# Layer 1 of a two-layer decoder step in two token groups, and the sample group's value sums in two fp32r passes over split pages

## The chip, the cores and the metric

The kernel runs on one core of one Trainium2 chip. The metric is device time in microseconds of one execution, input and output in HBM. The time before is 2708.54 us, the median of three runs (2706.16 to 2709.74).

## The reference

One inference step of a two-layer causal decoder (model width 1024) for two request groups that share one set of weights: a prompt of 1024 tokens, and eight sample requests of eight tokens each (64 rows) that have 1024 past tokens in a paged cache of keys and values (8 pages of 128 tokens per request, found through a page table). All data is fp32.

```python
for layer in range(DEPTH):                       # 2 layers
    hn = rms_norm(h, norm_mix_g[layer])
    if layer % 2 == 0:   # conformer convolution (width 31) | stick-breaking attention, 8 heads x 64
        mix = conformer_sb_mixer(hn, ...)        # w_in_even 1024 x 2560, w_out_even 1024 x 1024
    else:                # gated convolution (width 3) | causal pooling, windows 2/4/8/16
        mix = shortconv_pool_mixer(hn, ...)      # w_in_odd 1024 x 2048, w_out_odd 1024 x 1024
    h = h + mix
    h = h + swiglu(rms_norm(h, norm_ffn_g[layer]), w_ffn_in[layer], w_ffn_out[layer])   # 2816 wide
y = rms_norm(h, norm_final_g)

# stick-breaking attention of one block of queries
z = einsum('nqhd,nkhd->nhqk', q, k) * scale + bias
mask = k_pos < q_pos
log_1m = where(mask, log_sigmoid(-z), 0)
after = lax.cumsum(log_1m, axis=3, reverse=True) - log_1m
wgt = exp(where(mask, log_sigmoid(z) + after, -inf))
out = einsum('nhqk,nkhd->nqhd', wgt, v)
```

It also returns the new keys and values and the last rows of every convolution and pooling input.

## The kernel before

**Layout.** The residual stream lies in SBUF as `hb`, 128 channels by 8 blocks by 1088 token columns (1024 prompt, 64 sample). `Grp` names a set of columns and the width of one matmul: GA is the prompt's columns 0 to 511, one matmul of 512; GB the columns 512 to 1087 with the sample group at the end, two matmuls of 288; GT all 1088, three matmuls of 364, 364 and 360.

**Projections.** A product of fp32 numbers is made of fp32r numbers: every operand is split into a high part and a remainder, and `mm3` (L167) adds high x high, high x low and low x high, three passes per 128x128 block of the weight. Weights come as tiles of 512 KB (128 x 1024): `w_load` (L138) issues their DMAs on the SyncE queue into three `stage` buffers, `w_split` (L146) lets ScalarE (ACT) copy the high part (L152) and GpSimd (POOL) subtract for the low part (L153) into three `hl` buffers; both run a few tiles ahead of the matmuls. The list `seq` fixes the order of the tiles. A tile makes 8 x 3 = 24 passes (`block`, `pair`), or 4 x 2 x 3 in the second FFN matrix (`out_block`, L347). VectorE (DVE) takes the accumulators out: `scaled` (L226) multiplies by the norm's factor, `added` (L230) adds to `hb`. `run_in` (L280) runs an input projection with a function per output block, `run_out` (L315) an output projection that also prepares the next operand (`prep`, L302, with its low part on DVE at L307), `run_ffn` (L352) the SwiGLU. There `ev_u` gives a product to POOL (L378) and the split of the result to ACT and DVE (L175, L176) through `post`, a list that `flush` (L234) works off in the middle of the next block.

**Order.** The instructions are issued in the order of the program text, each engine's queue in order. Layer 0: the input projection for A, then for B (0 to 348 us); then output projection and FFN for A (348 to 1097), then for B (1097 to 1577). `to_mixer` (L1207) is the end of B's FFN: it adds the last products and prepares the operand of layer 1 for all 1088 columns. Layer 1 runs once for GT (1577 to 2658): input projection with its mixer (L1251 to L1353), output projection, FFN. `to_y` (L1366) ends the last FFN block by block with the final norm and the transposes to rows.

**Background.** Attention, convolution and the sample group run between the matmuls of a projection. They are generators that give back control after each piece; the projections call a `slot` at fixed places (L248, L260, L385 to L388, L412), and `bg` (L266) then issues one piece of the list `flow`. In group A's layer 0 this is `flow_c` (L1157): attention of group B (`attention`, L756: scores, `s2` with the scans on DVE at L815 to L820, transposes at L830, sums at L839), then the convolution of B (`conv_b`, taps at L693) alternating with the sample group, then the norm of the convolution. `last_a` (L1180) ends A's FFN and first issues what is left of the flow without gaps (`drain`).

**The sample group** (`sample`, L870): units of two or three pages of one request; `trans` transposes the key pages (L928) and splits them (L931, L932), `score` multiplies (L951), `weights` scans, `weights_t` transposes the weights in nine blocks (L1000), and `pv` sums the values: one fp32 matmul per page (L1012) of 64 weight columns and 512 value columns, and one for the new tokens (L1018) per request. Keys come one page to a buffer, values two.

## Time and profile before

| what | value |
|---|---|
| median of three runs | 2708.54 us |
| profiled execution, whole | 2708.54 us |
| its span, first to last instruction | 2706.8 us |
| mean granted TensorE clock | 0.987 |
| TensorE matmul busy | 2603.3 us (96%) |
| DVE / ACT / POOL busy | 1212.3 / 868.3 / 1031.1 us |
| HBM read / written | 198.09 / 18.69 MB |

The page gives the busy time of every engine in one profiled execution. A group of instructions is named by its line in the kernel, its engine and its operation, with `out<-in` by the program's names, the number of records, the busy time, the mean of one record, and the idle time just before them with what ended it. An fp32 matmul leaves two records. Matmuls overlap in the array, so a record's duration is longer than the distance to the next start. PEld is the loading of stationary operands, which overlaps.

### The profile page before, as it was taken

The numbers are of one execution on the slowest core, as the hardware profiler recorded it, in microseconds if no ns is written. First come the engines' busy times: TensorE is split into PE (matmuls) and PEld (weight loads), VectorE is DVE, ScalarE is ACT, GpSimd is POOL, SyncE is SP. The second block draws the span as 40 slices with busy tenths as digits, with TensorE's granted clock in tenths as the row PEclk, the third lists the DMA queues.
The fourth block names the chain that finished last, engine by engine and source line by source line (L and its number), as shares of the span: only waits on it lengthen the run. The fifth ranks groups of instructions, "written<-read, shape, count | busy, mean of one in ns | idle before, by whom it ended". The sixth has DMA issues, their size and how long they took to land. (4 is left out here: it accounts for less than half of the span.)

```text
span 2706.8 us, 37823 instructions
## 1 busy us (share of the span) xinstructions
PE 2603.3 (96%) x15423; PEld 2365.3 (87%) x15423; DVE 1212.3 (45%) x1730; ACT 868.3 (32%) x1326; POOL 1031.1 (38%) x589
## 2 busy tenths in 40 slices
PE   8989998998999998999999989999999999999997
PEld 6788876887666656899999989999999999999997
DVE  4774776868677642322222243343122222222226
ACT  4436765653433323332222232132211111111112
POOL 5655243343333337464444442224222222222222
PEclk9999999999999999999999999999999999999999
DMA  6432231234444432422222221131111111111111
GB/s 198 123 96 78 66 99 40 62 90 133 144 137 146 120 110 70 136 86 86 79 86 87 79 91 47 43 106 47 39 48 39 47 47 40 48 47 40 47 39 67
DMA packets 293380, 218.75 MB, mean 81 GB/s; under 512 B 21505, under 2 KB 248961, under 8 KB 293192
## 3 DMA queue, kind: packets, MB, share of 16 engines
q1 hardware_dynamic: 293176, 216.33, 26.8%
q8 instruction: 122, 2.00, 0.3%
q14 instruction: 50, 0.41, 0.1%
q10 hardware_dynamic: 32, 0.01, 0.0%
HBM read 198.09 MB, written 18.69 MB: 80 GB/s over the span
## 5 line engine op out<-in xcount | busy, mean ns | idle before, releaser
L153 POOL TENSOR_TENSOR hl<-stage,hl 128x1024 fp32r<-128x1024 f32 x278 | 679.5, 2446 | 1209.9 <-ACT hl L152 816.6
L170 PE MATMUL acc<-x1t,hl 128*128 128x364 f32 (+1 forms) x4896 | 824.1, 330 | 7.1 <-DVE hb L230 6.5
L170 PEld LDWEIGHTS acc<-x1t,hl 128*128 128x128 f32 x4896 | 817.2, 189 | 9.2 <-ACT x1t L304 6.7
L170 PE MATMUL acc<-x,hl 128*128 128x288 f32 (+1 forms) x4704 | 804.3, 325 | 12.9 <-DVE hb L230 9.6
L170 PEld LDWEIGHTS acc<-x,hl 128*128 128x128 f32 x4704 | 690.8, 189 | 88.7 <-issue 39.6
L170 PE MATMUL acc<-hid,hl 128*128 128x364 f32 (+2 forms) x3024 | 530.4, 333 | 20.5 <-DVE hb L230 17.5
L170 PEld LDWEIGHTS acc<-hid,hl 128*128 128x128 f32 x3024 | 480.0, 190 | 58.4 <-DVE hb L230 23.2
L152 ACT ACTIVATE hl<-stage 128x1024 fp32r<-128x1024 f32 x278 | 292.1, 1054 | 585.9 <-PE acc L170 318.5
L226 DVE TENSOR_TENSOR tmp<-acc,rr 128x728 f32<-128x728 f32 (+2 forms) x230 | 160.6, 720 | 684.3 <-PE acc L170 681.6
L230 DVE TENSOR_TENSOR hb<-acc,hb 128x728 f32<-128x728 f32 (+2 forms) x368 | 255.3, 720 | 273.2 <-PE acc L170 272.2
L176 DVE TENSOR_TENSOR hid<-tmp,hid 128x512 fp32r<-128x512 f32 (+2 forms) x66 | 60.8, 921 | 201.8 <-ACT hid L175 201.6
L187 POOL TENSOR_TENSOR ss<-ss,tmp 128x512 f32<-128x512 f32 (+2 forms) x55 | 98.4, 1789 | 91.6 <-ACT tmp L186 89.3
L378 POOL TENSOR_TENSOR tmp<-tmp 128x512 f32<-128x512 f32 (+2 forms) x66 | 117.1, 1774 | 29.3 <-ACT tmp L366 28.2
L175 ACT ACTIVATE hid<-tmp 128x512 fp32r<-128x512 f32 (+2 forms) x66 | 53.4, 809 | 230.8 <-POOL tmp L378 230.8
L170 PE MATMUL acc<-x1a,hl 128*128 128x512 f32 x480 | 122.4, 408 | 3.7 <-POOL hl L153 2.3
L366 ACT ACTIVATE tmp<-tmp 128x576 f32<-128x576 f32 (+1 forms) x44 | 39.6, 900 | 256.1 <-DVE tmp L226 256.1
L170 PEld LDWEIGHTS acc<-x1a,hl 128*128 128x128 f32 x480 | 89.9, 191 | 27.1 <-POOL hl L153 3.8
L693 DVE SCALAR_TENSOR_TENSOR cacc<-ext,par,cacc 128x512 f32<-128x512 f32 x120 | 90.1, 751 | 2.3
L364 POOL TENSOR_TENSOR tmp<-tmp 128x512 f32<-128x512 f32 x22 | 31.7, 1439 | 120.3 <-ACT tmp L363 113.1
L839 PE MATMUL o<-wt,vrow 128*64 128x128 f32 x576 | 76.6, 278 | 0.4 <-ACT wt L831 0.4
L818 DVE TENSOR_TENSOR_SCAN q<-q,ones 128x384 f32<-128x384 f32 (+6 forms) x56 | 76.0, 1357 | 2.0
L655 DVE SCALAR_TENSOR_TENSOR cacc<-ext,par,cacc 128x512 f32<-128x512 f32 x100 | 75.4, 754 | 3.0
(222 smaller groups left out, 1880.2 us busy)
## 6 DMA issues: line engine op xcount, KB each, us to landing
stage<-in_w_ffn_in_dram SPq DMA_DIRECT2D x132, 512.0 KB
stage<-in_w_ffn_out_dram SPq DMA_DIRECT2D x66, 512.0 KB
stage<-in_w_in_even_dram SPq DMA_DIRECT2D x40, 512.0 KB
kst<-in_cache_k_dram SPq DMA_DIRECT2D x64, 256.0 KB
vst<-in_cache_v_dram SPq DMA_DIRECT2D x64, 256.0 KB
stage<-in_w_out_even_dram SPq DMA_DIRECT2D x16, 512.0 KB
stage<-in_w_in_odd_dram SPq DMA_DIRECT2D x16, 512.0 KB
park<-hb SPq DMA_DIRECT2D x16, 288.0 KB
```

The source lines that it names most:

```text
L152: act.activation(hl[:, 0], st, AF.Copy)
L153: pool.tensor_tensor(hl[:, 1], st, f32(hl[:, 0]), op=OP.subtract)
L170: pe.matmul(acc[:, b, :c1 - c0], w, x[:, xi, c0:c1], start=first and s == 0, stop=last and s == 2)
L176: dve.tensor_tensor(dst[:, 1], src, f32(dst[:, 0]), op=OP.subtract)
L187: pool.tensor_tensor(ss[:, g.cs], ss[:, g.cs], t[:, :g.n], op=OP.add)
L226: dve.tensor_tensor(d, a, r, op=OP.mult)
L230: dve.tensor_tensor(d, a, d, op=OP.add)
L378: pool.tensor_tensor(t[:, :n], t[:, :n], u[:, :n], op=OP.mult)
L655: dve.scalar_tensor_tensor(acc, i, w, acc, op0=OP.mult, op1=OP.add)
L693: dve.scalar_tensor_tensor(o, i, w, o, op0=OP.mult, op1=OP.add)
L818: dve.tensor_tensor_scan(e, e, ones[:, 0:1].to_broadcast([128, n - 128]), q[:, n - 128:n - 127], op0=OP.mult, op1=OP.mult)
L839: pe.matmul(o, vrow[h][:, j], w[:, j], start=j == 0, stop=j == i)
```

## The change

- **Groups.** GT is gone. Layer 1 runs for GA right after layer 0 of GA, then both layers for GB. The weights of layer 1 (16 + 8 + 66 tiles) stand in the list twice. `mixer1(g, slot)` is the old mixer for one group: for A it keeps the last rows of the convolution and pooling inputs (`ghalo`, `uhalo`) that B starts from. `to_mixer(g, slot)` prepares the operand for one group only.
- **Background.** `flow_c` starts at the same place, but `bg2` issues a piece at every second slot, and the slots of A's layer 1 (and those added to `run_in`) serve it too. The final norm of A's columns becomes a flow of its own (`flow_y`) between B's layer-0 matmuls; `to_y` does B's columns alone, in two blocks of 256 and 320.
- **Deferred work.** The low part of the FFN's split (L176) goes to a list `late` and is issued one flush later. The transposes of keys and values to rows (`rows_out`) are deferred by one flush. In `attention`, the low parts of keys and queries (L781, L784) move from DVE to POOL.
- **Sample group.** Value pages are loaded one to a buffer (three buffers, the first used for the new tokens) and split by ACT and POOL into `vhl` (two buffers). The transposed weights are split too, high and low side by side as 128 stationary columns, so two fp32r matmuls per page make all four products; the result has 128 rows, which the following selection adds up. The new tokens' values stand as high and low in 64 rows each, with one matmul. Key transposes and scores are issued by single head pairs, in three pieces per step instead of two large ones; the nine transposes of the weights in three pieces.

```diff
+        for j, c in ODD:
+            add_in(w_in_odd[0], j * 512 + c * 128)
+        for n in range(8):
+            add_in(w_out_odd[0], n * 128)
+        add_ffn(1)
...
+    late = []
+
     def flush():
-        todo = post[:]
+        todo, low_parts = post[:], late[:]
         post.clear()
-        for f in todo:
+        late.clear()
+        for f in todo + low_parts:
             f()
...
             def fin():
                 pool.tensor_tensor(t[:, :n], t[:, :n], u[:, :n], op=OP.mult)
-                split(dst, t[:, :n])
+                act.activation(dst[:, 0], t[:, :n], AF.Copy)
+                late.append(lambda: dve.tensor_tensor(dst[:, 1], t[:, :n], f32(dst[:, 0]), op=OP.subtract))
             post.append(fin)
...
-                    small.append(lambda c=c: dve.tensor_tensor(k[o, c:c + 512], ks[:, c:c + 512],
+                    small.append(lambda c=c: pool.tensor_tensor(k[o, c:c + 512], ks[:, c:c + 512],
...
+            def split_v(upto):
+                while len(vhl) + vdone[0] < min(upto, 64):
+                    i = len(vhl) + vdone[0]
+                    v = vst.pop(i)
+                    t = vhl[i] = sa.tile([128, 2, 512], FR, name="vhl", bufs=2)
+                    act.activation(t[:, 0], v, AF.Copy)
+                    pool.tensor_tensor(t[:, 1], v, f32(t[:, 0]), op=OP.subtract)
+                    load_v(i + 4)
...
-                    act.activation(t[:, c0:c0 + n], m[:, :n * 128].rearrange("p (c r) -> p c r", r=128), AF.Copy)
+                    mv = m[:, :n * 128].rearrange("p (c b r) -> p c b r", b=2, r=64)
+                    o = wl[:, c0:c0 + n]
+                    act.activation(o[:, :, :, 0], mv, AF.Copy)
+                    dve.tensor_tensor(o[:, :, :, 1], mv, f32(o[:, :, :, 0]), op=OP.subtract)
+                    yield
...
-                pe.matmul(o, wts[bp][:, k, 64 * b2:64 * b2 + 64], vst[i // 2][:, k % 2], start=k == 0, stop=False)
-                if k % 2:
-                    vst.pop(i // 2)
-                    load_v(i // 2 + 3)
+                w = wts[bp][:, :, b2].rearrange("p c s r -> p c (s r)")
+                v = vhl.pop(i)
+                for s in range(2):
+                    pe.matmul(o, w[:, k], v[:, s], start=k == 0 and s == 0, stop=False)
+                vdone[0] += 1
+                split_v(i + 3)
...
+    def to_mixer(g, slot):
+        def f(hh):
+            for o in range(2):
+                h = w_next()
+                for i in range(4):
+                    n = o * 4 + i
+                    a = accs()
+                    out_block(g, a, h, i, hh)
+                    added(g, hb[:, n, g.cs], a)
+                    sp.dma_start(park[:, n, g.cs], hb[:, n, g.cs])
+                    prep(g, x1, n, pc(MIXG + 8 + n), squares=True)
+                    low(1)
+                    slot()
+            low()
+        return f
...
+    def bg2():
+        turn[0] += 1
+        if turn[0] % 2:
+            bg()
...
-    run_out(GA, accs, x1, FFNG, slot=bg)
+    run_out(GA, accs, x1, FFNG, slot=bg2)
+    ffn(GA, to_mixer(GA, bg2), True, bg2)
+    mixer1(GA, bg2)
+    run_out(GA, accs, x1, FFNG + 8, KS, slot=bg2)
...
+    ffn(GA, last_a, True, bg2)
...
+    flow.append(flow_y())
+    run_out(GB, accs, x1, FFNG, slot=bg2)
+    ffn(GB, to_mixer(GB, lambda: None), False, bg2)
+    drain()
+    mixer1(GB, lambda: None)
+    run_out(GB, accs, x1, FFNG + 8, KS)
...
+    ffn(GB, to_y, False, lambda: None)
```

More of the change, by code (lines that the diff above doesn't have):

```diff
@@ L73, in trunk_kernel @@
     gstack = ExitStack()
[L74 removed]
+    tmpp = gstack.enter_context(tc.tile_pool(name="tmpg", bufs=4, side="right"))
     def tmp():
[L77 removed]
+        return tmpp.tile([128, 640], F, name="tmp")
     ident = consts.tile([128, 128], F, name="ident")
@@ L122, in trunk_kernel @@
             add_in(w_in_even[0], 512 * j + c * 128)
+    ODD = [(j, c) for c in range(4) for j in (3, 1, 2, 0)]
     for _ in range(2):
@@ L287, in run_in @@
             end = i == len(evacs) - 3
-            block(g, a, h, x, ks if end else K0, flush)
+            block(g, a, h, x, ks if end else K0, flush, slot)
             if end:
@@ L293, in run_in @@
                 tail[1]()
+        flush()
         flush()
@@ L399, in run_ffn @@
             if q == G:
+                flush()
                 flush()
@@ L890, in sample @@
             pool.memset(f32(qb), 0.0)
-            vnew = sa.tile([128, 512], F, name="vnew")
-            pool.memset(vnew[64:128], 0.0)
+            vn = sa.tile([128, 512], FR, name="vn")
+            vnew = sa.tile([128, 512], F, name="vst", bufs=3)
             sp.dma_start(vnew[0:64], v_s.rearrange("a b q h d -> (a b q) (h d)"))
@@ L920, in trans @@
                 j = (2 * bp + b2) * 8 + 3 * kb
[L921 to L932 removed]
+                load_k(kpages.index(j) + n)
@@ L933, in trans @@
+                t = kth[u, pr, i] = sa.tile([128, 2, 384], FR, name="kth", bufs=2)
+                m = ms()
+                hp = 2 * pr + i
+                for pg in range(n):
+                    pe.transpose(m[:, pg * 128:pg * 128 + 128], kst[j + pg][:, hp * 128:hp * 128 + 128], ident)
+                act.activation(t[:, 0, :n * 128], m[:, :n * 128], AF.Copy)
+                dve.tensor_tensor(t[:, 1, :n * 128], m[:, :n * 128], f32(t[:, 0, :n * 128]), op=OP.subtract)
                 if i and pr:
@@ L1038, in sample @@
             fill_q(0)
-            load_v(2)
             for _ in range(6):
                 yield 1
-            for i in range(2):
-                trans(*steps[0], i)
-                yield 1
+            act.activation(vn[0:64], vnew[0:64], AF.Copy)
+            dve.tensor_tensor(vn[64:128], vnew[0:64], f32(vn[0:64]), op=OP.subtract)
+            split_v(1)
+            split_v(2)
             s = 0
-            while s < len(steps) or chain or pvq or fins:
+            while s <= 3 * len(steps) or chain or pvq or fins:
                 todo = fins[:] + chain.pop(s, [])
@@ L1103, in in_proj @@
             slot()
+        flush()
         flush()
@@ L1151, in trunk_kernel, with ffn @@
+    def ffn(g, last, sig, slot):
+        with tc.tile_pool(name=f"hid{g.c0}", bufs=2, side="right") as hidp:
+            run_ffn(g, accs, ms, hidp, x1, last, sig=sig, slot=slot)
     acc_pool(GA, 3)
-    hstack = ExitStack()
-    hidp = hstack.enter_context(tc.tile_pool(name="hid0", bufs=2, side="right"))
     knew = consts.tile([128, 4, NS], F, name="knew")
@@ L1360, in trunk_kernel, with flow_y @@
-    run_out(GT, accs, x1, FFNG + 8, KS)
+    def flow_y():
+        with tc.tile_pool(name="ya", bufs=1) as yp:
+            y = yp.tile([128, 4, D], F, name="ya")
+            gall = yp.tile([128, D], F, name="galla")
+            sp.dma_start(gall, bass.AP(tensor=norm_final_g.tensor, offset=norm_final_g.offset, ap=[[0, 128], [1, D]]))
+            yield 1
+            norm_cols(ms, D, 0, 4)
+            yield 1
+            for n in range(8):
+                m = ms()
+                for t in range(4):
+                    pe.transpose(m[:, t * 128:t * 128 + 128], hb[:, n, t * 128:t * 128 + 128], ident)
+                dve.tensor_tensor(y[:, :, n * 128:n * 128 + 128], m.rearrange("p (t c) -> p t c", t=4),
+                                  gall[:, None, n * 128:n * 128 + 128].to_broadcast([128, 4, 128]), op=OP.mult)
+                yield 1
+            for t in range(4):
+                act.activation(y[:, t], y[:, t], AF.Copy, scale=rstd[:, t:t + 1])
+                sp.dma_start(y_p[0, t * 128:t * 128 + 128], y[:, t])
+                yield 1
@@ L1425, in to_y @@
         LAG = 2
-        for q in range(24 + LAG):
-            if q < 24:
+        for q in range(16 + LAG):
+            if q < 16:
                 item(q)
             if q >= LAG:
-                turn(q - LAG)
-            if q % 8 == 4 and q > 8:
-                finish(q // 8 - 1)
-        finish(2)
-    with tc.tile_pool(name="hid1", bufs=2) as hidp:
-        run_ffn(GT, accs, ms, hidp, x1, to_y)
+                turn_y(q - LAG)
+            if q == 12:
+                finish(0)
+        finish(1)
```

472 lines of the change are left out of this document (219 added, 253 removed).

## The prediction

> **What bounds it now.** I read the page's busy shares first, then the stages, cut where the projections change their token group (header: busy per engine with instruction count, granted TensorE clock, DMA share, GB/s).
>
> ```profile
> PE 2603.3 (96%) x15423; PEld 2365.3 (87%) x15423; DVE 1212.3 (45%) x1730; ACT 868.3 (32%) x1326; POOL 1031.1 (38%) x589
> ```
> ```profile
> core 0: us, PE busy (x) PEld busy (x) DVE busy (x) ACT busy (x) POOL busy (x), PEclk, DMA share, GB/s
> 0.00:347.80 347.80, 323.45 (x1931) 278.12 (x1931) 214.72 (x318) 183.55 (x325) 181.89 (x145) 0.99 0.38 110
> 347.80:1096.60 748.80, 694.84 (x3260) 512.66 (x3257) 505.87 (x736) 336.00 (x593) 291.16 (x180) 0.97 0.37 108
> 1096.60:1576.90 480.30, 472.04 (x3567) 470.66 (x3567) 142.09 (x184) 135.31 (x161) 237.78 (x115) 1.00 0.30 89
> 1576.90:2657.60 1080.70, 1077.18 (x6437) 1070.15 (x6437) 317.16 (x410) 195.86 (x217) 302.87 (x133) 1.00 0.16 48
> 2657.60:2706.80 49.20, 35.78 (x234) 33.69 (x234) 32.48 (x83) 17.59 (x31) 17.35 (x18) 0.90 0.24 91
> ```
>
> TensorE sets the time in every row. The second is layer 0 of group A (512 columns) with the background flow between its matmuls: attention of B, B's convolution, the sample group. There TensorE stands idle 748.80 - 694.84 = 54.0 us, and a clock of 0.97 costs 0.03 x 748.8 = 22 us more. The third (layer 0 of B) and fourth (layer 1, all 1088 columns) idle 8 and 4 us. So only removed TensorE work, or those 54 + 22 us, can pay.
>
> **Layer 1 in two groups** replaces, for each 128x128 weight block and pass, three matmuls (364, 364, 360 columns) by one of 512 and two of 288. Starts in the timeline give the price of each, and the 360-wide groups the number of passes:
>
> ```profile
> 1042.51 15.64 PE L170 MATMUL acc<-x,hl 128*128 128x512 f32 x66
> 1057.98 1.56 PE L170 MATMUL acc<-hid,hl 128*128 128x512 f32 x6
> ...
> 1215.28 25.54 PE L170 MATMUL acc<-x,hl 128*128 128x288 f32 x192
> 1240.66 12.64 PE L170 MATMUL acc<-hid,hl 128*128 128x288 f32 x96
> ...
> 2007.99 48.15 PE L170 MATMUL acc<-x1t,hl 128*128 128x364 f32 x288
> 2055.98 24.16 PE L170 MATMUL acc<-hid,hl 128*128 128x364 f32 x144
> ```
> ```profile
> L170 PE MATMUL acc<-x1t,hl 128*128 128x360 f32 x1632 | 534.3, 327 | 0.0
> L170 PE MATMUL acc<-hid,hl 128*128 128x360 f32 x480 | 157.8, 329 | 0.0
> ```
>
> A 512 costs 15.47/66 = 0.2344 us, a 288 25.38/192 = 0.1322, a GT matmul 47.99/288 = 0.1666. New: 0.2344 + 2 x 0.1322 = 0.4988; old: 3 x 0.1666 = 0.4999. Over 1632 + 480 = 2112 passes: **-2.3 us**. The narrower matmuls themselves bring nothing.
>
> It loads and splits 16 + 8 + 66 = 90 weight tiles once more:
>
> ```profile
> L153 POOL TENSOR_TENSOR hl<-stage,hl 128x1024 fp32r<-128x1024 f32 x278 | 679.5, 2446 | 1209.9 <-ACT hl L152 816.6
> ```
>
> That is 90 x 2.446 = 220 us of POOL and 47 MB. A tile feeds 24 passes, 5.6 us of TensorE in A and 6.3 in B, so one 2.45 us split is covered: **0**. Without cover it would be these 220 us; in A the POOL also splits 64 value pages (an estimate from this row: half the elements, 1.2 us each, 78 us), well inside its idle time. SP carries the same number of page loads; each waits for a buffer, with weight loads queued behind it, but those run three buffers ahead. **0**, bound below under the rivals.
>
> **Value sums.** A page now takes one fp32 matmul, seen as two records:
>
> ```profile
> 973.01 1.93 PE L1012 MATMUL o<-vst,wts 128*64 128x512 f32 x4
> 974.87 1.67 PE L170 MATMUL acc<-x,hl 128*128 128x512 f32 x6
> ...
> 981.69 1.02 PE L1018 MATMUL o<-vnew,wts 128*64 128x512 f32 x2
> 982.64 1.66 PE L170 MATMUL acc<-x,hl 128*128 128x512 f32 x6
> ```
>
> Two pages take 1.86 us, one 0.93. After: two fp32r passes, whose nearest row is the 512-wide one, 2 x 0.234 = 0.469; saved 0.46 x 64 pages = 29.5. The new tokens: 0.95 to 0.234, eight times, 5.7. **-35.2 us**; bounds -35 and 0, the latter if the passes wait for their splits.
>
> **The background at half the density.** Counted in the code: before, 280 slots in group A's layer 0, each taking one of the flow's 271 pieces. After, A's two layers give 645 slots, every second takes a piece: 322 turns for 285 pieces (the sample loop's steps are finer). The flow ends inside A's last FFN; nothing is left for the drain. What TensorE waited for in the second stage:
>
> ```profile
> PE acc L170 <- DVE hb L230: 26.9, 8, 7.4
> PE m L1000 <- ACT wts L1001: 9.5, 4, 3.7
> PE m L830 <- DVE be L820: 7.5, 5, 3.5
> PE acc L170 <- DVE tmp L226: 2.1, 2, 1.1
> ```
>
> L1000: nine transposes through two PSUM tiles in one piece. They become three pieces: **-9.5**. L830: attention's scans are late; with twice the matmuls between pieces **-6**. The longest L230 wait:
>
> ```profile
> 439.41 5.09 POOL L153 TENSOR_TENSOR hl<-stage,hl 128x1024 fp32r<-128x1024 f32 x2 [0.86 <-ACT hl L152]
> 439.50 5.55 DVE L781 TENSOR_TENSOR kt<-kall,kt 64x512 fp32r<-64x512 f32 x2
> 445.91 4.61 PE L170 MATMUL acc<-x,hl 128*128 128x512 f32 x10 [7.38 <-DVE hb L230]
> ```
> ```profile
> 440.80:451.00 10.20, 5.09 (x12) 4.05 (x13) 8.48 (x6) 3.66 (x5) 6.58 (x4) 0.50 0.35 103
> ```
>
> Two key splits on DVE last as long as two weight splits on POOL, and the accumulator's release queues behind them. The change puts key and query splits on POOL, in order with the weight splits: **-7.4**. The clock then stays at 0.50 for 10.2 us, so a long wait costs about as much again. The Trainium skill's page "TensorE: Matmul & The Clock Gate" (section "What's actually happening") says the same: half clock until about 3.4 us of sustained work. By that price alone a 7.4 us wait would cost 1.7 us more, against the trace's 5.1; I stay with the trace.
>
> The end of A's FFN:
>
> ```profile
> 1068.98 2.34 POOL L153 TENSOR_TENSOR hl<-stage,hl 128x1024 fp32r<-128x1024 f32 x1
> ...
> 1073.24 0.69 DVE L176 TENSOR_TENSOR hid<-tmp,hid 128x512 fp32r<-128x512 f32 x1 [8.77 <-ACT hid L175]
> ...
> 1074.59 10.70 PE L170 MATMUL acc<-hid,hl 128*128 128x512 f32 x36 [5.68 <-DVE hb L230]
> ```
>
> DVE waits for ACT, which waits for POOL behind a weight split; the releases stand behind L176. The change issues L176 one flush later, when its input is long there. Of what is left of the first row (26.9 - 7.4 = 19.5) and the last (2.1) I take **-16**. Sum -39 of 54 idle; the clock share goes with it: **-16** of 22. Bounds for both together: 0 and -76.
>
> **What it adds.** Group A now goes through the layer change and the layer-1 mixer with the background running. In the layer change (old one, B to all columns):
>
> ```profile
> 1565.33 0.75 DVE L230 TENSOR_TENSOR hb<-acc,hb 128x576 f32<-128x576 f32 x1
> 1566.00 1.85 DVE L307 SCALAR_TENSOR_TENSOR x1t<-hb,par,x1t 128x1088 fp32r<-128x1088 f32 x1
> 1576.88 17.03 PE L170 MATMUL acc<-x1t,hl 128*128 128x364 f32 x90 [6.46 <-DVE hb L230]
> ```
>
> DVE's 0.75 + 1.85 = 2.6 a row block exceeded TensorE's 12 x 0.132 = 1.58; it ended in a 6.5 us wait, with half clock about 10. In B now 0.75 + 1.85 x 576/1088 = 1.73: the old 10 becomes 5, **-5**. In A 0.69 + 0.87 = 1.56 and every second block a background piece (1.7 us of DVE, below) make 2.4, against 6 x 0.234 = 1.41 and the piece's 0.4: eight blocks x 0.6 and some half clock, **+7** (bounds 0 and 10, as before). The mixer:
>
> ```profile
> L226 DVE TENSOR_TENSOR tmp<-acc,rr 128x512 f32<-128x512 f32 x54 | 37.1, 687 | 60.2 <-PE acc L170 57.9 <-POOL tmp L364 2.1
> L1255 DVE TENSOR_TENSOR hb<-hb,tmp 128x1088 f32<-128x1088 f32 x4 | 11.5, 2880 | 0.1
> L1294 DVE SCALAR_TENSOR_TENSOR hb<-ext,par,hb 128x1024 f32<-128x1024 f32 x8 | 10.2, 1279 | 0.0
> L693 DVE SCALAR_TENSOR_TENSOR cacc<-ext,par,cacc 128x512 f32<-128x512 f32 x120 | 90.1, 751 | 2.3
> L693 DVE SCALAR_TENSOR_TENSOR hb<-ext,par,hb 128x64 f32<-128x64 f32 x120 | 52.4, 437 | 3.0
> L932 DVE TENSOR_TENSOR kth<-m,kth 128x384 fp32r<-128x384 f32 x64 | 35.0, 552 | 33.3 <-ACT kth L931 33.3
> ```
>
> At 512 columns a channel tile costs DVE 4 x 0.69 + 1.36 (L1255 scaled) + 3 x 0.64 (L1294 halved) + about 4.5 pooling and split operations at 1.0, midway from L176's 0.69 to 1.36: 10.5, four make 42. The 63 slots take 31 pieces: 15 with convolution taps (2 x 0.75 + up to 3 x 0.44, say 2.5) = 38, and 0.5 (L932) in each for the sample = 16. TensorE: the second stage without idle, clock loss and its 8 + 66 tiles (748.8 - 54 - 22 - 74 x 5.63) is 256, less the 35 saved 221, over 271 pieces 0.82 each; 16 x 5.63 + 31 x 0.82 = 115. DVE at 96 of 115, and ACT and DVE queues in order: I take **+15** (bounds 0 and, with two-operand work doubled, +27). Two more changes from one projection to the next under background: **+3**. B's mixer has two sets of waits where there was one: **+3**. In the first 348 us and the tail nothing that sets the end changes.
>
> **Sum** on the profiled span: 2706.8 - 2.3 - 35.2 - 39 - 16 + 7 - 5 + 15 + 3 + 3 = 2637.3. The profiled execution took 2708.5 (1.7 outside the span), which is the median of the runs: **2639 us**, 2.6% faster.
>
> **Rivals.**
>
> *Nearly no stalls* (chance 0.14). The new +7 and +15 do not come, slots being sparse; 2639 - 22 = 2617, and with the rest of the idle 2600. For: B's layer 0 idles 8 us in 480. Against: DVE at 0.83 in the mixer.
>
> *Stalls only move* (0.15). The waits and clock loss stay, -39 - 16 is not earned: 2694. For: 26.9 of the 54 us are releases behind an in-order DVE queue, which the new schedule keeps.
>
> *Value passes wait* (0.07). Each waits for ACT and POOL to split its page behind a weight split; the 35 us turn into waits: 2674.
>
> *Slower: DVE held by POOL* (0.08). At 439.50 two operations of two SBUF operands took 5.55 us where L176 of as many columns takes 0.69 alone, some 1.9 us more each. In A's mixer some 38 such (L1255, L1294, pooling, splits) run while POOL is busy about half the time, and 16 more at the layer changes: 54 x 1.9 = 103, less 115 - 96 = 19 of slack and the +15 already counted: +69, and some 15 of half clock after the long waits: 2723. It decides where DVE passes TensorE's 115 us there, that is, once the two-operand work (42 - 11 = 31) grows by 60%. For: L1255 takes 2.65 ns an element. Against: L1294, with two SBUF operands too, takes 1.25. The Trainium skill's page "GPSIMD Engine Reference" (section "8. Key points") speaks for it: GpSimd shares its SBUF interfaces with VectorE and contends with instructions of two SBUF inputs; the trace agrees at 439.50.
>
> *The change doesn't do as it says*: the flow not used up before the drain, at 2.6 us a piece at most; the count leaves 37 turns over, so it goes into the moving stalls.
>
> **Numbers.** The forecast (2620 to 2665) has 0.52, the rivals the chances above, and 0.04 lies between 2703 and 2714. Some 0.2% is what a measurement of this kernel can tell from no change. Faster 0.88, same 0.04, slower 0.08. The range 2590 to 2697 leaves out the slow rival, no change, and a mixer that costs nothing with all idle gone.
>
> **What would show it.** Page: fp32 value records (128 + 16) gone, 136 matmuls 512 wide at 0.23 us apart; POOL up by some 300 us. Stages: B's two layers near 1.00 clock; A's about 1190 us (2637 less the first 348, B's 162 x 24 x 0.264 + 30, and a tail of 40). Waits: L1000 and the 7.4 and 5.7 us L230 waits gone. Wrong if a wait on DVE above 20 us in total appears in A's mixer, if releases by the page split (POOL) stand ahead of value passes, or if A's clock is still 0.97.

## The result: 0.46% slower

The changed kernel takes 2720.97 us (median of five runs, 2718.35 to 2722.16), the kernel before 2708.54 (here also a median of five): a ratio of 1.0046, 95% interval 1.0031 to 1.0061. Forecast were 2639 us. The profiled execution of the changed kernel took 2720.97 us, its span is 2719.1. One execution of the experiments below, of e4, took 5022 us and is left out of e4's figures. The page's first part:

```profile
PE 2570.9 (95%) x15415; PEld 2289.1 (84%) x15415; DVE 1309.2 (48%) x1810; ACT 1019.4 (37%) x1619; POOL 1417.9 (52%) x838
```

TensorE has less to do than before (busy 2570.9 after 2603.3), and all three other engines more: POOL 387 us, ACT 151, DVE 97. The stages of the changed kernel, with the columns of the prediction's table; A's two layers are rows two to six:

```profile
core 0: us, PE busy (x) PEld busy (x) DVE busy (x) ACT busy (x) POOL busy (x), PEclk, DMA share, GB/s
0.00:353.90 353.90, 324.95 (x1931) 279.71 (x1931) 214.81 (x302) 184.35 (x326) 202.51 (x161) 0.98 0.37 109
353.90:932.00 578.10, 551.00 (x2742) 445.50 (x2742) 380.06 (x450) 270.15 (x445) 314.04 (x196) 0.99 0.34 98
932.00:959.00 27.00, 19.78 (x74) 15.54 (x75) 21.04 (x29) 13.70 (x25) 15.88 (x11) 0.82 0.43 139
959.00:1107.00 148.00, 121.78 (x549) 96.74 (x549) 83.45 (x146) 60.41 (x121) 62.08 (x43) 0.96 0.37 109
1107.00:1587.00 480.00, 463.51 (x2045) 371.67 (x2046) 248.79 (x363) 179.02 (x289) 313.58 (x178) 0.98 0.37 109
1587.00:1612.90 25.90, 10.52 (x35) 6.45 (x34) 15.73 (x16) 9.42 (x16) 9.95 (x7) 0.77 0.41 121
1612.90:2100.60 487.70, 484.06 (x3612) 482.88 (x3612) 144.87 (x196) 132.31 (x157) 226.26 (x108) 0.99 0.29 88
2100.60:2687.40 586.80, 575.70 (x4286) 572.38 (x4286) 181.16 (x256) 158.84 (x221) 263.96 (x125) 1.00 0.29 86
2687.40:2719.10 31.70, 19.57 (x146) 18.20 (x146) 19.28 (x58) 11.22 (x21) 9.67 (x12) 0.86 0.21 75
```

Against the prediction's own stages: the first part takes 353.9 for 348, A's two layers 1612.9 - 353.9 = 1259.0 for about 1190 (its terms give 1193), B's two layers 487.7 + 586.8 = 1074.5 for 1056, the tail 31.7 for 40. So **66 to 69 of the 82 us missing lie in A's two layers**. There TensorE stands idle 1259.0 - 1166.6 = 92 us (the five PE busy times add up to 1166.6), and the clock costs 578.1 x 0.01 + 27.0 x 0.18 + 148.0 x 0.04 + 480.0 x 0.02 + 25.9 x 0.23 = 32 us more. In A's layer 0 before it was 54 and 22. The prediction wanted the two to shrink by 55; with A's layer 1 and its background they grew by 48. (This clock share also counts half clock in which TensorE stood idle. Counted on TensorE's busy time alone, in slices of 0.5 us, it is 22 us, 15 before, and the growth 45.) Three short stretches stand out: the change of layers (932 to 959, clock 0.82), A's mixer (959 to 1107), and A's last sums (1587 to 1613, TensorE busy for 10.5 of 25.9 us).

What TensorE waited for, in the whole run (microseconds in total, number of waits, the longest):

```profile
PE acc L169 <- DVE hb L229: 55.4, 26, 9.1
...
PE acc L169 <- DVE hid L384: 5.4, 3, 4.4
...
PE z L807 <- POOL kt L787: 4.7, 1, 4.7
```

The wait for the nine weight transposes (9.5 us before) is gone, as forecast. The wait for accumulators that `added` has not yet taken out (now L229) has grown from 33.6 us in ten waits to 55.4 in 26, on average 2.1 us.

The longest of them is the one that the prediction meant to remove. The timeline where it stands, at the end of A's first output projection (start, length, engine, line, operation; in brackets the idle time before and what ended it):

```profile
417.39 3.42 POOL L787 TENSOR_TENSOR kt<-kall,kt 64x512 fp32r<-64x512 f32 x2
...
417.88 6.23 DVE L311 SCALAR_TENSOR_TENSOR x<-hb,par,x 128x512 fp32r<-128x512 f32 x3
...
421.10 5.20 POOL L152 TENSOR_TENSOR hl<-stage,hl 128x1024 fp32r<-128x1024 f32 x2 [0.29 <-POOL kt L787]
...
424.03 2.56 DVE L821 TENSOR_TENSOR_SCAN q<-q,ident 128x128 f32<-128x128 f32 x1
426.62 1.82 DVE L824 TENSOR_TENSOR_SCAN q<-q,ones 128x768 f32<-128x768 f32 x1
...
429.55 1.28 DVE L229 TENSOR_TENSOR hb<-acc,hb 128x512 f32<-128x512 f32 x2
...
430.38 1.19 PE L169 MATMUL acc<-x,hl 128*128 128x512 f32 x2 [9.11 <-DVE hb L229]
```

The key splits are on POOL now (L787), but DVE's next operations of two SBUF operands, `prep`'s low parts (L311), take their place: three of them last 6.23 us while POOL works through two key splits and two weight splits (3.42 and 5.20 us, 0.29 between). Behind them stand the scans of attention, and only then the release. The 7.4 us wait became 9.1.

### The profile page after: what moved, and what is told of

It reads as the page before. It is cut to its first block, busy times and chain, and to the rows that moved or that the text cites. A ratio compares the mean times of both kernels' runs of the same rounds, so it can differ in the third digit from the quotient of the medians.

```text
span 2719.1 us, 38898 instructions
## 1 busy us (share of the span) xinstructions
PE 2570.9 (95%) x15415; PEld 2289.1 (84%) x15415; DVE 1309.2 (48%) x1810; ACT 1019.4 (37%) x1619; POOL 1417.9 (52%) x838
## 5 line engine op out<-in xcount | busy, mean ns | idle before, releaser
L169 PE MATMUL acc<-x,hl 128*128 128x288 f32 (+1 forms) x9600 | 1648.8, 329 | 39.2 <-DVE hb L229 25.8
L169 PEld LDWEIGHTS acc<-x,hl 128*128 128x128 f32 x9600 | 1450.6, 190 | 170.9 <-issue 30.5
L152 POOL TENSOR_TENSOR hl<-stage,hl 128x1024 fp32r<-128x1024 f32 x368 | 896.3, 2438 | 847.9 <-ACT hl L151 616.3
L169 PE MATMUL acc<-hid,hl 128*128 128x288 f32 (+1 forms) x3072 | 542.3, 333 | 34.9 <-DVE hb L229 29.5
L151 ACT ACTIVATE hl<-stage 128x1024 fp32r<-128x1024 f32 x368 | 386.0, 1053 | 418.2 <-PE acc L169 208.9
L169 PEld LDWEIGHTS acc<-hid,hl 128*128 128x128 f32 x3072 | 466.4, 189 | 89.6 <-DVE hb L229 38.6
L225 DVE TENSOR_TENSOR tmp<-acc,rr 128x512 f32<-128x512 f32 (+1 forms) x230 | 166.1, 723 | 726.2 <-PE acc L169 722.3
L229 DVE TENSOR_TENSOR hb<-acc,hb 128x512 f32<-128x512 f32 (+1 forms) x376 | 268.1, 721 | 257.0 <-PE acc L169 256.5
L186 POOL TENSOR_TENSOR ss<-ss,tmp 128x512 f32<-128x512 f32 (+1 forms) x69 | 100.1, 1451 | 115.5 <-ACT tmp L185 114.6
L382 POOL TENSOR_TENSOR tmp<-tmp 128x512 f32<-128x512 f32 (+1 forms) x88 | 119.8, 1361 | 17.8 <-ACT tmp L370 17.5
L384 DVE TENSOR_TENSOR hid<-tmp,hid 128x512 fp32r<-128x512 f32 (+1 forms) x88 | 81.1, 922 | 19.7 <-ACT hid L383 19.7
L699 DVE SCALAR_TENSOR_TENSOR hb<-ext,par,hb 128x64 f32<-128x64 f32 x120 | 87.8, 732 | 3.0
L311 DVE SCALAR_TENSOR_TENSOR x<-hb,par,x 128x576 fp32r<-128x576 f32 (+1 forms) x56 | 74.8, 1355 | 19.9 <-ACT x L308 19.9
```

What stands on the lines that cost most here:

```text
L151: act.activation(hl[:, 0], st, AF.Copy)
L152: pool.tensor_tensor(hl[:, 1], st, f32(hl[:, 0]), op=OP.subtract)
L169: pe.matmul(acc[:, b, :c1 - c0], w, x[:, xi, c0:c1], start=first and s == 0, stop=last and s == 2)
L186: pool.tensor_tensor(ss[:, g.cs], ss[:, g.cs], t[:, :g.n], op=OP.add)
L225: dve.tensor_tensor(d, a, r, op=OP.mult)
L229: dve.tensor_tensor(d, a, d, op=OP.add)
```

## The experiments

Two theories. **Theory 1**: the loss sits at a few places of group A where TensorE, DVE, ACT and POOL take turns in order, each with its own cause. **Theory 2**: it is one cause, POOL's added load, which holds DVE wherever the two work at once. Times below are medians; "to before" is the difference to the kernel before on the same chip (2708.2 to 2710.4 us there), in which the changed kernel has +12.4.

| kernel | us | to before | ratio, 95% interval |
|---|---|---|---|
| changed kernel | 2720.97 | +12.4 | 1.0046 [1.0031, 1.0061] |
| e1 before + new sample group | 2725.72 | +17.1 | 1.0062 [1.0045, 1.0079] |
| e2 A's squares moved | 2711.43 | +2.8 | 1.0009 [0.9999, 1.0019] |
| e3 mixer without background | 2694.73 | -13.9 | 0.9941 [0.9924, 0.9957] |
| e4 a piece at every slot | 2741.82 | +33.2 | 1.0112 [1.0092, 1.0132] |
| e5 key, query splits on DVE | 2710.69 | +1.7 | 1.0004 [0.9994, 1.0014] |
| e6 page splits on DVE | 2733.67 | +24.6 | 1.0093 [1.0076, 1.0110] |
| e7 layer change without background | 2711.40 | +2.4 | 1.0008 [0.9998, 1.0018] |
| e8 before + new key schedule | 2734.67 | +25.6 | 1.0096 [1.0079, 1.0113] |
| e9 e2, e3, e5, e7 together | 2675.19 | -34.5 | 0.9870 [0.9855, 0.9886] |
| e10 e9 + last pairs without background | 2668.16 | -41.5 | 0.9844 [0.9831, 0.9858] |
| e11 changed, old sample group | 2728.90 | +19.3 | 1.0074 [1.0059, 1.0089] |
| e12 changed, no page remainders | 2711.46 | +1.1 | 1.0007 [0.9997, 1.0017] |
| e13 e10, old sample group | 2695.98 | -12.2 | 0.9950 [0.9931, 0.9969] |
| e14 e10 + norm without background | 2669.57 | -38.6 | 0.9861 [0.9845, 0.9878] |

### The places: e3, e2, e7, e4

```diff
-    mixer1(GA, bg2)                            # e3
+    mixer1(GA, lambda: None)
```

> The changed kernel with no background in A's layer-1 mixer; its 31 pieces are issued later, in the same density. Theory 1 (the queues of the mixer and of the background block each other there): the stretch shrinks from 148 to some 100 us, the pieces cost 25 us later, 2695 to 2700. Theory 2: the pieces bring their waits along, 2715 to 2721.

Measured 2694.73, 26.3 us below the changed kernel: theory 1's number (0.3 us under its range). The mixer's stage in e3:

```profile
959.00:1060.00 101.00, 96.64 (x404) 75.77 (x403) 47.18 (x71) 32.68 (x50) 48.23 (x33) 0.98 0.31 94
```

Alone it needs 101 us with DVE busy for 47; with 31 pieces of background it took 148 with DVE busy for 83. DVE was not full there. TensorE stands idle 148.0 - 121.8 = 26.2 us in it, in many short waits, of which these are four:

```profile
PE z L963 <- DVE kth L945: 5.0, 1, 5.0
PE acc L169 <- DVE x L175: 4.0, 1, 4.0
...
PE m L1321 <- DVE kth L945: 2.8, 2, 1.7
PE m L193 <- DVE kth L945: 2.5, 1, 2.5
```

The sample group's key splits (`kth`) end 10.3 us of them; the rest are the mixer's own operations and other pieces of the sample group. Without background (e3) TensorE is idle for 4.4 us, 4.0 of them in one wait for the norm. The longest of the changed kernel:

```profile
998.39 1.54 DVE L1261 SCALAR_TENSOR_TENSOR hb<-ext,par,hb 128x512 f32<-128x512 f32 x2
...
999.49 2.64 POOL L152 TENSOR_TENSOR hl<-stage,hl 128x1024 fp32r<-128x1024 f32 x1 [2.56 <-issue]
...
999.85 3.36 DVE L992 TENSOR_TENSOR_SCAN qf<-qf,ones 128x512 f32<-128x512 f32 x1
...
1003.13 0.53 DVE L945 TENSOR_TENSOR kth<-m,kth 128x384 fp32r<-128x384 f32 x1
...
1003.72 0.69 PE L963 MATMUL z<-kth,qb 128*128 128x384 f32 x1 [5.03 <-DVE kth L945]
```

The score matmul stands in TensorE's queue only two pieces behind its key split; the split waits on DVE behind the mixer's convolution and a scan, TensorE waits with it, and the mixer's own matmuls wait behind the score. The scan takes 3.36 us beside POOL's weight split; the shortest of its kind takes 1.28. So theory 2's hold on DVE has a part in this place too.

```diff
                 added(GA, hb[:, n, GA.cs], a)
-                add_squares(GA, hb[:, n, GA.cs], n == 0)      # e2: last_a
...
             yield 1
+            for n in range(KC):                               # flow_y, beside B's matmuls
+                add_squares(GA, hb[:, n, GA.cs], n == 0)
+                yield 1
             norm_cols(ms, D, 0, 4)
```

> The changed kernel with the squares of group A taken out of the end of A's second FFN and put, one a piece, ahead of the final norm in the flow that runs under B's first projection. Theory 1 (a ring in the end of the FFN: release, square on ACT, split on ACT, subtraction on DVE, release): that end gets some 11 us of idle time and 8 us of half clock back, 2700. Theory 2 (POOL holds DVE everywhere, no place of its own): the squares only move, 2715 to 2721.

Measured 2711.43, 9.6 us less: between the two expectations, the direction of theory 1 at half its size. Each block of `last_a` in the changed kernel is a ring of four operations:

```profile
1589.86 0.69 DVE L229 TENSOR_TENSOR hb<-acc,hb 128x512 f32<-128x512 f32 x1
1590.58 0.63 ACT L185 ACTIVATE tmp<-hb 128x512 f32<-128x512 f32 x1 [1.43 <-DVE hb L229]
...
1591.12 0.67 ACT L174 ACTIVATE x<-hb 128x576 fp32r<-128x576 f32 x1
...
1591.82 1.37 DVE L175 TENSOR_TENSOR x<-hb,x 128x576 fp32r<-128x576 f32 x1 [1.27 <-ACT x L174]
1593.11 0.68 DVE L229 TENSOR_TENSOR hb<-acc,hb 128x512 f32<-128x512 f32 x1
...
1593.84 1.67 PE L169 MATMUL acc<-hid,hl 128*128 128x512 f32 x6 [1.51 <-DVE hb L229]
```

One turn lasts 1593.11 - 1589.86 = 3.25 us, for 1.4 us of matmuls. The square (L185) stands between `added` and the split that B's operand needs, and nothing else is in flight: the clock is 0.77 over these 26 us. L175 takes 1.37 us here beside POOL's sum of the squares and 0.76 just before, so a part of what e2 gains is DVE being held less.

```diff
-    ffn(GA, to_mixer(GA, bg2), True, bg2)      # e7
+    ffn(GA, to_mixer(GA, lambda: None), True, bg2)
```

> The changed kernel without the 8 background slots in group A's change from layer 0 to layer 1 (the four pieces move to later slots). Theory 1: the stretch from 932 to 959 us, 27.0 us long at a clock of 0.82, gets 6 to 12 us shorter and the time is 2709 to 2715. Theory 2: the pieces cost the same wherever they are done, and the time is 2718 to 2722.

Measured 2711.40, 10.0 us less: theory 1's number. The first wait of the layer change is still there in e7, 4.45 us long as in the changed kernel:

```profile
930.93 2.88 DVE L699 SCALAR_TENSOR_TENSOR hb<-ext,par,hb 128x64 f32<-128x64 f32 x3
931.05 2.35 POOL L152 TENSOR_TENSOR hl<-stage,hl 128x1024 fp32r<-128x1024 f32 x1
933.72 0.69 DVE L384 TENSOR_TENSOR hid<-tmp,hid 128x512 fp32r<-128x512 f32 x1
934.46 2.50 PE L169 MATMUL acc<-hid,hl 128*128 128x512 f32 x5 [4.45 <-DVE hid L384]
```

L384 is the low part that the change issues one flush later (L176 before). At the end of A's first FFN it comes last, behind convolution taps that are held until POOL's weight split is done, and TensorE waits for it.

```diff
     def bg2():
         turn[0] += 1
-        if turn[0] % 2:                        # e4
-            bg()
+        bg()
```

> The changed kernel with a piece at every slot of A, as before, so that the flow ends within A's layer 0 and layer 1 runs without background. Theory 1 (half density helps under the FFN, but the mixer and the change of layer lose more): mixer and layer change free, the waits of the dense stretch back: 2690 to 2710. Theory 2 (time with POOL and DVE both loaded is what counts, wherever it lies): no change, 2715 to 2725.

Measured 2741.82, 20.7 us more, worse than either theory had it. Theory 1 expected the gain of a mixer that the flow no longer reaches; but at full density the waits of the scores for key splits come to 30 us, after 5.0 in the changed kernel. So the prediction's step on density holds in this direction: half is better than full.

### Which engine: e5, e6, e12

```diff
-                    small.append(lambda c=c: pool.tensor_tensor(k[o, c:c + 512], ks[:, c:c + 512],
+                    small.append(lambda c=c: dve.tensor_tensor(k[o, c:c + 512], ks[:, c:c + 512],
...
-                small.append(lambda: pool.tensor_tensor(qz[hh][r], qs, f32(q[r]), op=OP.subtract))
+                small.append(lambda: dve.tensor_tensor(qz[hh][r], qs, f32(q[r]), op=OP.subtract))
```

> The changed kernel with one part of the change undone: the second parts of the prompt's keys and queries (the tiles kt and qz) are made on DVE again instead of POOL. The prediction gave that move 7.4 us. Theory 1 (A's stage loses at a few places where TensorE, ACT, DVE and POOL take turns in order, whichever of DVE and POOL has the operation): the 9.1 us wait at 421 us changes by less than 3 us and the time is 2717 to 2725. The prediction's own reason (the move frees DVE): the time is 2726 to 2730. Theory 2 (DVE is held wherever POOL works, so less work on POOL is worth time): 2708 to 2716.

Measured 2710.69, 10.7 us less than with these splits on POOL: the time is theory 2's, the wait at 421 us (8.2 us here) stays as theory 1 had it, and the prediction's term has the wrong sign. The operation by itself, in the changed kernel and in e5 (minimum, median, maximum in ns):

```profile
L787 POOL TENSOR_TENSOR kt<-kall,kt x24: 1257/1282/2716, 239.7 to 607.4; 64x512 fp32r<-64x512 f32 x24
```
```profile
L787 DVE TENSOR_TENSOR kt<-kall,kt x24: 675/686/2790, 236.4 to 594.9; 64x512 fp32r<-64x512 f32 x24
```

POOL takes 1.9 times as long, and its weight splits queue behind. Most of the cost lies in a place that the prediction had left out, A's own attention before 348 us: the matmuls of A's first output projection start at 355.3 us in the changed kernel and at 348.2 in e5. In the changed kernel the first score of A's attention waits 4.7 us for its key split on POOL (L807 in the list of waits above); in e5 it waits 2.9 us for another operand. The same 70 us ahead of it, changed kernel and e5:

```profile
230.00:300.00 70.00, 61.96 (x425) 55.05 (x424) 43.74 (x53) 47.84 (x100) 37.26 (x43) 0.95 0.23 62
```
```profile
230.00:300.00 70.00, 65.84 (x459) 58.69 (x457) 52.64 (x70) 50.85 (x108) 25.97 (x34) 0.98 0.23 64
```

425 matmuls against 459: with the splits on DVE, 3.9 us more of TensorE's work fit in. The long wait at the end of the output projection is 8.2 us in e5, so neither engine removes it.

```diff
                     act.activation(t[:, 0], v, AF.Copy)
-                    pool.tensor_tensor(t[:, 1], v, f32(t[:, 0]), op=OP.subtract)
+                    dve.tensor_tensor(t[:, 1], v, f32(t[:, 0]), op=OP.subtract)      # e6; e12 leaves the line out
```

> The changed kernel with the subtraction of the 64 value pages on DVE instead of POOL. POOL loses 64 operations, DVE gains 64 of 512 elements. Theory 2 (DVE is held by POOL's operations on two operands): DVE's operations get shorter than what it gains, the 64 wide taps fall from 732 ns towards 437 ns, and the time is 2700 to 2714. Theory 1 (the losses sit at the layer change, in the mixer, in the last sums of A and at the ends of the output projections): the time is 2719 to 2730, since DVE has more in its queue at these places.

> The changed kernel without the 64 subtractions of the value pages' second parts on POOL; both passes of a value sum read the first part, so the part of the sums that the second parts carry is left out and TensorE's passes stay as many. Nothing is given to DVE in exchange, other than where these subtractions were put on DVE (+12.7 us). Theory 2 (POOL's load holds DVE and costs time wherever it is): DVE's taps get shorter than 732 ns and the time is 2695 to 2711. Theory 1 (a few places of A where the engines take turns): the subtractions lie beside other work except in the mixer, and the time is 2713 to 2721.

e6: 2733.67, 12.2 us more, above both expectations. e12: 2711.46, 11.3 us less, between the two expectations and 0.5 us from theory 2's. The narrow convolution taps show what POOL does to DVE: changed kernel, e6, e12:

```profile
L699 DVE SCALAR_TENSOR_TENSOR hb<-ext,par,hb 128x64 f32<-128x64 f32 x120 | 87.8, 732 | 3.0
```
```profile
L928 DVE TENSOR_TENSOR vhl<-vst,vhl 128x512 fp32r<-128x512 f32 x64 | 76.0, 1192 | 22.5 <-ACT vhl L927 22.0
L699 DVE SCALAR_TENSOR_TENSOR hb<-ext,par,hb 128x64 f32<-128x64 f32 x120 | 60.4, 504 | 3.0
```
```profile
L699 DVE SCALAR_TENSOR_TENSOR hb<-ext,par,hb 128x64 f32<-128x64 f32 x120 | 77.8, 649 | 3.0
```

The mean of the 120 taps is 437 ns before the change and 732 after it. It is not that each gets slower: in all four kernels the shortest takes 271 to 277 ns and the median 285, and single ones take up to 2.3 or 2.5 us, held until an operation of POOL is done. With more on POOL more of them are held. Taking 64 subtractions off POOL gives DVE back 10 to 27 us of taps, so theory 2's mechanism is there; but given to DVE they cost it 76 us, three times what the taps gave back. And the gain of e12 lies in one place: its profiled execution is 7.8 us shorter than the changed kernel's, and over the 768 matmuls from the start of A's mixer through the output projection and the first eight tiles of the FFN it has 274.1 us, the changed kernel 282.1. The Trainium skill's page "Perfetto Trace Analysis" (section "Optimizing Scalar/DVE Operations") warns that moving operations between GpSimd and VectorE might not help, as they share a read port; e5 and e6, where the move to DVE gave 10.7 us and cost 12.2, agree with its "might".

### The sample group by itself: e1, e8, e11

e1 is the kernel before with the change's `sample` and nothing else of it; e8 has of that only the keys: split by single head pairs into two small buffers, scored in three pieces per step, with the old fp32 value sums. e11 is the changed kernel with `sample` of the kernel before.

```diff
-                if s + 1 < len(steps):                        # e1, e8; e11 the other way round
-                    trans(*steps[s + 1], 0)
...
+                st, piece = divmod(s, 3)
+                if piece == 0 and 0 < st <= len(steps):
+                    score(*steps[st - 1], 1)
...
+                if piece < 2 and st < len(steps):
+                    trans(*steps[st], piece)
+                if piece == 2 and st < len(steps):
+                    score(*steps[st], 0)
```

> The kernel before with the new sample group alone (value pages split, two fp32r passes, finer pieces), all else as it was. By the sum of the prediction (35.2 us of TensorE less, the waits at L1000 of 9.5 us gone): about 2665. If the value passes wait for their splits: 2700 to 2710. If the page splits on POOL hold DVE up in this dense background: above 2710.

> The kernel before with the new key schedule alone: key splits by half steps in two buffers, scores two pieces behind their split instead of four or five; the value sums stay one fp32 pass over pages as loaded. It tells apart what made the kernel before with the whole new sample group 2725.7 us. If the shorter lead of the keys is at fault: the waits of the scores for their key splits stay near 30 us, and the time is 2730 to 2745. If the page splits' load on POOL and DVE is at fault: these waits fall under 8 us and the time is 2704 to 2715.

> The changed kernel with the sample group of the kernel before (fp32 value sums, keys split a step ahead): the other half of the change, both layers in two groups with the places of the background that go with it. The new sample group alone made the kernel before 17 us slower. If that loss comes with the new sample group wherever it stands, this kernel is at 2721 - 17 = 2704 or below (2696 to 2708). If the new sample group does earn its 35 us of TensorE time here, where its key waits are 8 us and not 36, the time is 2735 to 2756.

e1 is 17.1 us slower than before. The stretch of the sample group holds as many matmul records in both, before and e1:

```profile
600.00:1009.00 409.00, 391.12 (x1687) 269.59 (x1687) 281.51 (x510) 144.61 (x297) 136.14 (x70) 0.98 0.45 135
```
```profile
600.00:1030.00 430.00, 369.35 (x1689) 293.61 (x1688) 330.71 (x538) 183.20 (x385) 214.90 (x133) 0.94 0.43 129
```

The waits of TensorE in e1:

```profile
PE z L957 <- DVE kth L946: 17.1, 9, 3.8
PE z L957 <- DVE kth L939: 13.4, 12, 3.9
PE z L957 <- ACT kth L938: 5.2, 3, 4.1
```

TensorE is busy 22 us less and idle 43 us more, 36 of them in waits of the scores for their key split, of which the kernel before has none among its longest. Its time is the third that was expected (above 2710), but the next kernel shows that the page splits are not needed for the loss. With the key schedule alone (e8, 2734.67) the time is worse still, 25.6 us above before, as expected of the shorter lead, though these waits come to 15 us there and not 30:

```profile
PE z L948 <- DVE kth L930: 8.6, 7, 3.9
...
PE z L948 <- DVE kth L937: 6.5, 3, 3.7
```

The score matmuls, as many in both, are busy for 52.9 us in e8 and 38.1 before. So the new value sums, with the weight transposes in three pieces, are worth 8.5 us in this frame (e8 to e1), and the new key schedule costs three times that. (e1 and e8 have 285 pieces for the old 280 slots; the few left over are issued without cover at the end of A's FFN, which is a part of their loss. No run separates it from the shorter lead.) e11 gives 2728.90, between its two expectations: the new sample group brings the changed kernel 6.9 us, where the two groups alone cost 19.3. Neither half of the change is faster by itself. The stretch from the first matmul of A's mixer to the reload of its last operands takes 154.5 us in the changed kernel, with TensorE idle for 28 at a clock of 0.95, and 143.1 in e11, idle for 14 at 0.99: half of the idle time there comes with the new sample group, most of the rest with the background as such (e3 has 4.4 us left).

### Together: e9, e10, e13, e14

e9 has the edits of e2, e3, e5 and e7. e10 adds:

```diff
         a0, a1 = pair(g, accs, x, K0, {k: [lambda k=k: prep(g, x, k, pc(gcol + k)), lambda: low(0)]
-                                       for k in range(6)}, slot)
+                                       for k in range(6)})
...
-    ffn(GA, last_a, True, bg2)
+    ffn(GA, last_a, True, bg3)                 # bg3: also at every tenth turn
```

> The changed kernel with four edits at once: no background pieces in group A's mixer and none in its change of layers, the squares of A's last sums moved into B's part, and the prompt's second parts of keys and queries on DVE again. If the four causes are separate places (theory 1), their gains add up: 2721 - 26 - 9.5 - 9.6 - 10 = 2666, so 2660 to 2673, faster than the kernel before by 1.3 to 1.8 per cent. If they share one cause, a total load on POOL and DVE that is only moved about (theory 2), the gains don't add up and the time is 2680 to 2695, where the mixer's edit alone has it.

> The four edits, and in both of group A's output projections no background pieces in the last pair of blocks; the 7 pieces that this moves are done in A's second feed-forward block, which takes a sixth piece at every fifth turn. Theory 1: the wait at the end of the first output projection (9.1 us near 421 us) and that of the second (5.6 us near 1168 us) go, with the half clock behind the first: 10 to 20 us, so 2646 to 2660. Theory 2: no more than 4 us beside the four edits.

e9: 2675.19. Singly the four edits bring 26.3 + 9.6 + 10.0 + 10.7 = 56.6 us, together 46.9, 2 us above theory 1's range: mostly separate places. e10: 2668.16, 7 us more, less than theory 1 and more than theory 2 had. It is **1.56% faster than the kernel before** (0.9844, 0.9831 to 0.9858). What TensorE waits for in e10:

```profile
PE acc L169 <- DVE tmp L225: 10.8, 5, 3.8
...
PE acc L169 <- DVE hb L229: 8.7, 7, 1.8
```

The releases that cost 55.4 us cost 8.7. The first row, scaled blocks at the start of a stage, led to e14, which leaves the first two blocks of each FFN without background too (A's first FFN takes `bg3` in exchange):

```diff
-                        run_in(g, accs, x, [ev_g, lambda a: ev_u(0, a)], norm_hooks(g, ps), slot=slot)
+                        run_in(g, accs, x, [ev_g, lambda a: ev_u(0, a)], norm_hooks(g, ps))
```

> The five edits, and no background pieces in the first two blocks of the feed-forward stages, where the norm is made; A's first feed-forward stage takes the sixth piece at every fifth turn in exchange. If the waits for the norm (3 us at its spread, 3.8 us for the first scaled blocks, at each of A's two stages) come from pieces ahead of it on DVE: 2654 to 2663. If they are the norm's own length: 2665 to 2671, no change.

> The five edits with the sample group of the kernel before (fp32 value sums, keys split a step ahead). It measures the term of 35.2 us that the prediction gave the new value sums, where most of the other places are mended. If the sums were right and only hidden by those places, this kernel is 30 to 38 us above the five edits, at 2698 to 2706. If the new sample group spends most of what its matmuls save on shorter leads and more splits wherever it stands (it brought 8 us in the changed kernel and lost 17 in the one before), it is 2672 to 2685.

e14: 2669.57, its interval lies across e10's: no change, as expected if these waits are the norm's own length. e13, the five edits with the old sample group: 2695.98, 29 us above e10 (a little under the range expected if the sums were right). Where the places are mended, the whole new sample group earns 29 of the 44.7 us that the prediction gave it (35.2 for the value sums, 9.5 for L1000); in the changed kernel as it is, 7. The matmuls themselves save what the sum says: from the start of a page's value sum to the next matmul it is 0.96 us on average before and 0.51 after.

## Why the prediction was wrong

**Right.** The removed work: 0.96 - 0.51 = 0.45 us a page, 0.46 in the prediction's sum of 35.2. What the new sample group earns in the end is 29 of 44.7 (e13 to e10); the rest goes to its key steps, which the sum priced only by their number. L1000's 9.5 us went, and most of L830's: A's two layers have 1.3 left. The page splits cost POOL 1.34 us each (1.2 estimated), and in the changed kernel the value passes never waited for them (5.3 us in e1). B's layer change waits 1.8 us after 6.5. The flow's last operation ran at 1482 us, before A's last sums.

**Layer 1 in two groups, -2.3.** It brought nothing. In the changed kernel's timeline of TensorE, clean stretches of 288-wide passes:

```profile
1764.44 12.96 PE L169 MATMUL acc<-hid,hl 128*128 128x288 f32 x96
...
1956.44 8.83 PE L169 MATMUL acc<-hid,hl 128*128 128x288 f32 x65
```

192.00 us for the 1440 passes between these starts are 0.1333 us each, not 0.1322. A 512-wide one takes 0.2333 (78.40 us for 336, from 1470.87 to 1549.27), so the three make 0.4999, as the old three did. The same 1.1 ns on the 4512 passes of 288 that the kernel before had are 5 us more. Why the passes got 1% longer is open: the kernels with the old layer 1 have 0.132, all with the new one 0.133, also in B's layer 0, whose projections the change leaves as they were.

**The idle time of A's stage, -39, and its clock, -16: the step that failed.** The prediction took the waits of the second stage one by one and let the new order remove most: 15 us idle were to be left. In A's two layers, outside the layer change, the mixer and the last sums, TensorE still idles 27.1 + 16.5 = 44 us. Three parts of the step fell. Moving the key splits to POOL (-7.4) was costed by whom the wait named, not by what the operation does on the other engine: 1282 ns instead of 686, in POOL's queue, with the next operations of two operands held in the same place. It cost 10.7 us (e5). The releases (-16) did not come earlier by issuing L176 a flush later: at the end of A's first FFN TensorE now waits 4.45 us for that very operation, where the release behind it took 5.68 before. Nor did half the density remove them. Of the 53.5 us in A's two layers, 14.7 lie at the ends of the output projections, 4.8 in the layer change and 15.3 in the last sums, up to B's first matmul. In e10, where these places take *no* piece and A's squares are gone, 6.9 are left in A. The other 18.7, sixteen shorter waits in the FFNs' second matrix, also fall there, though pieces still run beside it; why is not shown. And the clock did not come back, because the idle did not go. Its price was too high as well: of the 10.2 us at half clock around the 7.4 us wait TensorE worked for 5.1 and so lost 2.5, not about as much as the wait.

**The mixer, +15 with a bound of +27: mis-sized, and by the wrong measure.** 16 x 5.63 + 31 x 0.82 = 115 us of TensorE work is about right (121.8 busy). It took 148 us, 33 more. The prediction asked whether DVE's total (96 of 115) fits; DVE's total was 83 of 148. What counts is how long the one operation stands in the queue that TensorE's next instruction waits for. The sample group's scores had a lead of two pieces, and half of the idle time goes with the old sample group (e11). That the lead was cut from a step to two pieces stands in the change; the prediction costed the key steps at nothing but their count. Without background the mixer's stage is 101 us, and the kernel gains 26.3.

**The layer change, +7:** 10.0 by e7, at its upper bound; its first wait, for L384, is not among them. **The tail and the last sums, nothing:** moving A's squares into `last_a` was passed over. It cost 9.6 us (e2), with no cover, since `drain` has emptied the flow there.

**The first 348 us, nothing:** 353.9. The moved key splits serve A's attention as well as B's; the same edit, another stage.

The slow rival was near in its time (2723) but not in its mechanism: DVE did not pass TensorE's time in the mixer (83 of 122 us of matmuls). POOL's hold on DVE is real. Leaving out the page splits' subtractions gives 11.3 us (e12), but that also shortens POOL's own queue, so how much of it is the hold stays open. (Its size of 1.9 us an operation was 2.1 by its own row, (5.55 - 2 x 0.69) / 2.) Of the prediction's signs of being wrong one came: over A's two layers the clock is still 0.97. The waits on DVE in A's mixer add up to 18.8 us, just under its 20. Nearest in mechanism was "stalls only move" (2694): it had the waits stay, not grow by 45 to 48 us.

**What stays open.** The five edits gain 53.9 us, but the prediction had already allowed 22 for two of the places. Against its terms they show 11 us in the mixer, 3 in the layer change, 10 in the squares, 18 in the key splits (+10.7 for -7.4) and 7 at the ends of the output projections: 49 of the 82, and some 10 less where they are taken together. The sample group earns 16 less than its terms, and longer 288-wide passes take some 7. About 10 to 20 us are left that no run here places.

## What to carry to other kernels

A wait that comes of several engines taking turns in order goes away when nothing else is queued there; spreading the other work thinner did not remove it here. So leave the layer changes, mixers and last sums free of background, and put it into the long even stages. (The Trainium skill's page "Perfetto Trace Analysis", section "Optimization Strategy", says that interleaving regimes may pay. Here moving the pieces of the mixer to other stages gained 26 us; no run leaves the FFN stages without them.) Before an operation changes its engine, price it there, with what is queued behind it and every stage that uses the line; and when a pipeline is cut into finer steps, count how far ahead of its reader each operand is made, because a saving in matmuls turns into waits when that lead goes.

## What was not expected of the hardware

- A busy POOL holds some DVE operations for whole microseconds and leaves others alone. The 64-column taps, with both operands in SBUF, went from 437 to 732 ns in the mean at an unchanged median of 285. The 512-column taps of the same line, whose sum lies in PSUM, kept 751 ns in both kernels. No run separates the width from the place of the sum.
- Half clock outlasts the wait. Around the 9.1 us wait that ended at 430.4 us the granted clock was 0.50 from 423.4 to 433.6; around the 3.9 and 7.2 us waits that ended at 1602.8 and 1612.9 it was 0.50 from 1601 to 1618, although TensorE worked without a break from 1612.9 on. With the squares moved (e2) the half clock there lasted from 1598.7 to 1602.
- The distance between equal 288-wide passes differs by 1% between programs, 132.0 and 133.3 ns in the mean, throughout a kernel.
